# When a gather may start, and whose bytes its rows land in: a hold and a buffer choice in a hybrid encoder block

## The chip, the cores and the metric

One core of one Trainium2 chip runs the whole program. The engines are PE (TensorE: matmuls; its weight loads are listed apart as PEld), DVE (VectorE), ACT (ScalarE), POOL (GpSimd, which also issues the indirect gathers) and SP (SyncE, which issues most other DMAs). Each engine works through its own instructions in a fixed order. The metric is the time of the program on the device, in microseconds; lower is better.

## The reference, cut to what matters

```python
h_res = concat([meta, x])                     # 16 + 1024 tokens of 1024 features
hn = _rmsnorm(h_res, norm_mix)
z = hn @ w_in                                 # all projections
y_m = _mlstm(...)                             # 4 heads of 128, chunk by chunk with a carried state
y_f = _forgetting_attention(...)              # 8 heads of 64
h_res = h_res + concat([y_m, y_f]) @ w_out    # then the 16 meta tokens are dropped
# PEER, for each token, with x = _rmsnorm(h_res, norm_ffn):
#   scores against 2 x 128 keys for each of 8 heads, top 16 of each, top 16 of their pairs
#   -> ids: 8 x 16 = 128 experts of 16384, gate: softmax of their scores
u = u_emb[ids]
act = gelu(einsum('ted,td->te', u, xb))
w = gate * act
out = h_res + einsum('te,ted->td', w, v_emb[ids])
```

Everything is float32.

## The kernel before, in words

The 1024 tokens are cut into four segments of 256 tokens, each of two blocks (A and B) of 128. Each segment passes its projections (`proj`), the mLSTM (`mlstm`), the attention (`fox`), the output projection and the norm (`outp`), and the choice of experts (`topk`: q projection, scores, top 16; eight heads, one after the other, each writing 16 columns of the index tile `idx` and of `gate`). What this text calls the front of a segment is the part up to `outp`. The last instructions of `outp` transpose the normed tokens (`xT`, L858).

The experts are evaluated in two ways. Segments 1 and 2 (512 tokens) are done densely: every expert row is multiplied with every token (`dense_u`, L293, and `dense_v`, L1258), and the gates are scattered into a matrix over all experts (`gates`: 128 groups of four tokens, with one-hot rows A on DVE and ACT, one-hot rows B on POOL and DVE at L1161, their product `gout` on PE at L1163, a copy to `G` on ACT at L1165, and a store `gd`). Segments 0 and 3 gather: for each block, 128 gathers fetch one u row per token each (`gu`, L329: 128 tokens by 1024 floats, 512 KB), DVE (L338) or POOL and ACT (L335, L336) multiply a row with the tokens `xng` and sum it; `weigh` makes the weights with gelu and gate; then 128 gathers, one per token, fetch that token's 128 v rows (`gv`, L365), and `po` (L387) multiplies four of them at a time on PE. Such four gathers are called a four.

`gather_items` gives the order for a gathered segment: all of A's u rows; then in turn a four of A's v rows and four of B's u rows; then B's v rows. `GS0` says which of 16 u rows are multiplied on POOL: rows 2, 5, 8, 11, 14 for block A and none for block B.

A gathered row lands in a buffer of one of two pools. `gp` has 7 and is open from the start. `gpv` has 4; it takes the bytes that the mLSTM's tiles (`vp`, `og`, `mqk`) use, and opens once the mLSTM of the last segment is done. `room0` chooses for segment 0 (L1004): a v row of block A goes to `gpv` from the four with number JV on, one of block B in every second four, all else to `gp`.

The instructions of a program are put in order for each engine by a planner that runs them on a model of the chip ahead of time; among instructions that could go it takes the one that stands first in the program. The gather of segment 0 stands late in the program (`GP0` = 5: after the gates), so its instructions fill what the others leave. In the kernel before, `gather` adds a dependency by hand: the first gather waits for `segs[1].done`, the last transpose of segment 1's `outp`, and all other gathers of the segment are put behind the first.

The program runs in stages. Stage i has the mLSTM of segment i, then, merged, its attention and output projection, the projections of segment i + 1, in stage 1 the top-k of segment 0, and in stage 3 that of segments 1 and 2. After stage 3 come, merged, the top-k of segment 3, part of the dense u products (`spill`) and the gates. The dense phase follows, with the gather of segment 3 paced beside it.

Of the kernel before, what the change touches and what calls it, by code (L numbers as in the profile page):

```python
# [19 lines left out]
P = 128  # L20
# [60 lines left out]
GATH = 7  # L81
GATHV = 4

JV = 4

RATE = 1.08
LAG = 5
# [6 lines left out]
def _block_kernel(ctx, tc, nc, I, out, dbg):  # L94
# [30 lines left out]
    def bank(name):  # L125
        turn_b[0] += 1
        if extra is not None and turn_b[0] % XB == 0:
            return extra[:, turn_b[0] // XB % 2, :]
        return ps.tile([P, 512], F32, tag="bank", name=name, bufs=2)
# [9 lines left out]
    dve, act, pe, pool_e, sync = nc.vector, nc.scalar, nc.tensor, nc.gpsimd, nc.sync  # L139
# [6 lines left out]
    ident = identr.bitcast(F32)  # L146
# [67 lines left out]
    def rsqrt(o, x, scale, t):  # L214

        act.activation(o, x, AF.Ln, bias=epsc[0:x.shape[0]], scale=scale)
        act.activation(o, o, AF.Exp, scale=-0.5)
        act.activation(t, o, AF.Square)
        dve.scalar_tensor_tensor(t, x, EPS / scale, t, op0=OP.add, op1=OP.mult)
        dve.tensor_scalar(t, t, -0.5 * scale, 1.5, op0=OP.mult, op1=OP.add)  # L220
        dve.tensor_mul(o, o, t)
# [32 lines left out]
    def rawt(name):  # L254
        return wp.tile([P, L], F32, tag="raw", name=name, bufs=RAW)
# [8 lines left out]
    for i in range(3):  # L264
        c = slice(i * 512, min(L, i * 512 + 512))
        for e, t in enumerate((oz, zo)):
            t = t[0:NH_F, 0:c.stop - c.start]
# [130 lines left out]
    def gather_items(S, share, room):  # L398

        A, B = (gather_rows(S, lb, share[lb], room) for lb in range(NB))  # L400
        yield from A.u
        for i in range(0, P, 4):
            yield from A.v[i:i + 4]
            yield from B.u[i:i + 4]
        yield from B.v


    def segment(sg):
        S = SimpleNamespace()
        S.sg = sg  # L410
        S.idT = None
        S.nb = nb = SEGS[sg]
        S.xb0 = xb0 = sum(SEGS[:sg])
        S.off = off = NMETA if sg == 0 else 0
        S.nx = nb * P
        S.n = S.nx + off
        S.c0 = 0 if sg == 0 else NMETA + xb0 * P
        S.chunks = ([(0, NMETA)] if sg == 0 else []) + [(off + i * P, P) for i in range(nb)]
        S.hx = len(S.chunks) - nb
        S.xs = slice(xb0 * P, xb0 * P + S.nx)  # L420
        S.T1 = S.c0 + S.n
        return S

    def tok_proj(wsrc, xh, xl, tbs, consume):

        bks = [acc_bank("tk") for _ in tbs]
        for kp in range(4):
            if xl is None:
                raw = rawt("raw")[:, 0:1024]
                sync.dma_start(raw, wsrc[kp])  # L430
                for k in (2 * kp, 2 * kp + 1):
                    for b, (ti, (s0, w)) in zip(bks, tbs):
                        pe.matmul(b[0:w, :], xh[:, k, s0:s0 + w], raw[:, k % 2 * 512:(k % 2 + 1) * 512],  # L433
                                  start=(k == 0), stop=(k == KT - 1))
                continue
            for kk, (h, l) in enumerate(halves(wsrc[kp], SHARE)):
                k = 2 * kp + kk
                for b, (ti, (s0, w)) in zip(bks, tbs):
                    a, c = xh[:, k, s0:s0 + w], xl[:, k, s0:s0 + w]
                    for i, (x, wx) in enumerate(((a, h), (a, l), (c, h))):  # L440
                        pe.matmul(b[0:w, :], x, wx, start=(k == 0 and i == 0), stop=(k == KT - 1 and i == 2))
        for b, (ti, (s0, w)) in zip(bks, tbs):
            consume(ti, w, b)
# [376 lines left out]
    def outp(S):  # L820

        nb, xb0, yh, yl = S.nb, S.xb0, S.yh, S.yl
        if dbg: dbg("yh", S.sg, yh); dbg("yl", S.sg, yl)
        h2p = sp.tile([P, NB, D], F32, tag="u0", name="h2b")
        h2s = [h2p[:, b, :] for b in range(nb)]
        for b in range(nb):
            sync.dma_start(h2s[b], I["x"][(xb0 + b) * P:(xb0 + b + 1) * P, :])
        for nq in range(2):
            def take_w(ti, w, b):
                o = h2s[ti][:, nq * 512:(nq + 1) * 512]  # L830
                dve.tensor_add(o, o, b)
            tok_proj(I["wo"][nq], yh, yl, [(b, (b * P, P)) for b in range(nb)], take_w)
            yield
        gffn = rawt("gffn")[:, 0:D]
        sync.dma_start(gffn, I["g_ffn"].partition_broadcast(P))
        if S.sg <= DENSE[1]:
            half_ = slice((S.sg - DENSE[0]) % 2 * NX, ((S.sg - DENSE[0]) % 2 + 1) * NX)
            xh, xl = Xh[:, :, half_], Xl[:, :, half_]
        else:
            xh = hp.tile([P, KT, NTOK], F32R, tag="hh", name="xh3")[:, :, 0:nb * P]  # L840
            xl = None
        if S.sg in Q32:
            xh, xl = xh.bitcast(F32), None
        S.xh, S.xl = xh, xl
        for b in range(nb):
            gb_ = xb0 + b
            sync.dma_start(h2d[gb_ * P:(gb_ + 1) * P, :], h2s[b])
            xn = rawt("xn")[:, 0:D]
            ssq = sp.tile([P, 3], F32, tag="ssq", name="ssq")
            act.activation(xn, h2s[b], AF.Square, accum_out=ssq[:, 0:1])  # L850
            rsqrt(ssq[:, 1:2], ssq[:, 0:1], 1.0 / D, ssq[:, 2:3])
            dve.scalar_tensor_tensor(xn, h2s[b], ssq[:, 1:2], gffn, op0=OP.mult, op1=OP.mult)
            if S.sg not in DENSE:
                sync.dma_start(xnd[gb_ * P:(gb_ + 1) * P, :], xn)
            for half in range(2):
                tb = bank("xT")
                for i in range(4):
                    S.done = pe.transpose(tb[:, i * P:(i + 1) * P], xn[:, (4 * half + i) * P:(4 * half + i + 1) * P], ident)  # L858
                dsth = xh[:, 4 * half:4 * half + 4, b * P:(b + 1) * P]
                if xl is not None:  # L860
                    dstl = xl[:, 4 * half:4 * half + 4, b * P:(b + 1) * P]
                tbv = tb.rearrange("p (k t) -> p k t", k=4)
                act.copy(dsth, tbv)
                if xl is not None:
                    dve.tensor_sub(dstl, tbv, dsth.bitcast(F32))
        yield
# [111 lines left out]
    segs = [segment(i) for i in range(len(SEGS))]  # L978
    NPROJ, NTOP = 2 + 1 + 8 + 2 + 8, NH_P

    def main(S):
        yield from fox(S)
        yield from outp(S)
# [21 lines left out]
    def room0(kind, lb, i):  # L1005

        if kind == "v":
            return gpv if (i >= JV if lb == 0 else i % 2) else gp
        return gp

    def gather(S, share):
        first = None
        for ask, use in gather_items(S, share, room0):
            with tc.issue_after(first.ins) if first else nullcontext():
                t, d = ask()
            if first is None:
                first = d

                tc.add_manual_dep(d.ins, segs[1].done.ins.name, mybir.DependencyInfo(
                    mybir.DependencyClass.Sync, mybir.DependencyReason.DATA), reason="hold")  # L1020
            more = use(t)
            if more:
                more()

    class Paced:
# [22 lines left out]
        def use(self):  # L1048
            _, f, t = self.open.pop(0)
            with ExitStack() as es:  # L1050
                for k in ("pe", "dve"):
                    if k in seen:
                        es.enter_context(tc.issue_after(seen[k].ins))
                more = f(t)
            if more:
                self.later.append((self.at, more))
# [11 lines left out]
    def gather_first(at):  # L1068
        if GP0 == at:
            gather(segs[0], GS0)  # L1070

    for i in range(-1, len(SEGS)):
# [9 lines left out]
        if i >= 0:  # L1082
            S = segs[i]
# [239 lines left out]
```

## Time and profile before

| what | value |
|---|---|
| median of 3 runs | 3425.85 us (3422.84 to 3432.39) |
| the profiled execution | 3424.24 us, span 3422.4 us |
| mean granted clock of TensorE | 0.926 |
| PE, DVE, ACT, POOL busy | 3040.1, 2294.6, 1066.8, 1523.4 us |
| HBM read, written | 860.91 MB, 67.47 MB |

A line of the page or of an answer of the trace has the line of the kernel, the engine, the operation, the tiles (out<-in) and a count; `[... <-X]` or `<-X` names what ended the idle time before an instruction. In tables by stretch the first figures are the start, end and length of a stretch in microseconds from the start of the span; then each engine's busy microseconds, with the number of its records in brackets; then the granted clock of TensorE as a share of full speed, the mean busy share of the 16 DMA engines and the GB/s they moved. An answer for one tile counts all instructions that write or read it: for `gu` on DVE two records for each row (product and its sum), on POOL the gathers and POOL's own products.

### The profile page before, as it was taken

The numbers are of one execution on the slowest core, as the hardware profiler recorded it, in microseconds if no ns is written. First come the engines' busy times: TensorE is split into PE (matmuls) and PEld (weight loads), VectorE is DVE, ScalarE is ACT, GpSimd is POOL, SyncE is SP. The second block draws the span as 40 slices with busy tenths as digits, with TensorE's granted clock in tenths as the row PEclk, the third lists the DMA queues.
The fourth block names the chain that finished last, engine by engine and source line by source line (L and its number), as shares of the span: only waits on it lengthen the run. The fifth ranks groups of instructions, "written<-read, shape, count | busy, mean of one in ns | idle before, by whom it ended". The sixth has DMA issues, their size and how long they took to land. (4 is left out here: it accounts for less than half of the span.)

```text
span 3422.4 us, 42278 instructions
## 1 busy us (share of the span) xinstructions
PE 3040.1 (89%) x14225; PEld 2220.2 (65%) x14225; DVE 2294.6 (67%) x5970; ACT 1066.8 (31%) x2007; POOL 1523.4 (45%) x1321
## 2 busy tenths in 40 slices
PE   8899899878768868999998775999999999999999
PEld 4566677545535646676766553777777777777666
DVE  3242678577667999776788546788767677775443
ACT  1323424233333212222444553222322232322221
POOL 1000011177875777433565675454444545444442
PEclk9998899879679888999998886999999999999999
DMA  4444445579989999866787887888889999998995
GB/s 135 131 126 137 144 145 149 167 240 315 250 299 331 328 334 346 252 242 234 283 325 280 316 302 284 287 311 314 307 310 344 345 348 343 353 342 308 339 333 205
DMA packets 373821, 931.23 MB, mean 272 GB/s; under 512 B 57268, under 2 KB 143508, under 8 KB 371556
## 3 DMA queue, kind: packets, MB, share of 16 engines
q0 software_dynamic: 161216, 552.56, 45.9%
q1 hardware_dynamic: 212388, 375.96, 32.7%
q8 instruction: 113, 1.85, 0.2%
q14 instruction: 104, 0.85, 0.1%
HBM read 860.91 MB, written 67.47 MB: 271 GB/s over the span
## 5 line engine op out<-in xcount | busy, mean ns | idle before, releaser
L329 POOL DMA_INDIRECT gu<-in_peer_u,idx x512 | 626.3, 1223 | 521.1 <-PE vo L1258 110.0
L365 POOL DMA_INDIRECT gv<-in_peer_v,idT x512 | 546.0, 1066 | 593.1 <-PE po L387 314.3
L338 DVE SCALAR_TENSOR_TENSOR gu<-gu,xng 128x1024 f32<-128x1024 f32 x472 | 592.5, 1274 | 62.5 <-DMA gu<-in_peer_u,idx 60.6
L282 ACT CAST wh<-raw 128x1024 fp32r<-128x1024 f32 x288 | 302.1, 1049 | 884.2 <-PE vo L1258 270.9
L287 DVE TENSOR_TENSOR wl<-raw,wh 128x1024 fp32r<-128x1024 f32 x262 | 320.5, 1223 | 283.0 <-ACT wh L282 250.5
L1258 PE MATMUL vo<-wh,Wh 128*128 128x512 f32 x1024 | 376.7, 396 | 34.9 <-ACT Wh L1239 18.1
L1258 PE MATMUL vo<-wl,Wh 128*128 128x512 f32 x1024 | 402.6, 393 | 0.0
L1258 PE MATMUL vo<-wh,Wl 128*128 128x512 f32 x1024 | 400.3, 392 | 0.0
L387 PE MATMUL po<-gv,Z 128*32 128x512 f32 x2048 | 262.7, 606 | 19.1 <-DMA gv<-in_peer_v,idT 18.9
L306 PE MATMUL fp<-hnh,raw 128*128 128x256 f32 (+1 forms) x1024 | 251.4, 404 | 22.3 <-DVE frs L633 11.3
L1258 PEld LDWEIGHTS vo<-wh,Wh 128*128 128x128 f32 x1024 | 194.1, 190 | 98.3 <-issue 23.3
L293 PE MATMUL du<-xl,wh 128*128 128x512 f32 x640 | 250.3, 391 | 0.0
L293 PE MATMUL du<-xh,wl 128*128 128x512 f32 x640 | 250.2, 391 | 0.0
L293 PE MATMUL du<-xh,wh 128*128 128x512 f32 x640 | 249.8, 390 | 0.0
L306 PEld LDWEIGHTS fp<-hnh,raw 128*128 128x128 f32 x1024 | 203.8, 203 | 60.5 <-DVE frs L633 12.7
L1258 PEld LDWEIGHTS vo<-wl,Wh 128*128 128x128 f32 x1024 | 193.8, 189 | 48.6 <-issue 8.4
L1258 PEld LDWEIGHTS vo<-wh,Wl 128*128 128x128 f32 x1024 | 193.2, 189 | 48.1 <-issue 7.5
L1163 PE MATMUL gout<-A,B 128*128 128x128 f32 x1024 | 164.0, 319 | 67.6 <-POOL B L1161 62.9
L1163 PEld LDWEIGHTS gout<-A,B 128*128 128x128 f32 x1024 | 150.9, 226 | 103.6 <-POOL B L1161 76.6
L1165 ACT COPY G<-gout 128x512 f32<-128x512 f32 x128 | 136.4, 1066 | 202.0 <-PE gout L1163 195.4
L433 PE MATMUL tk<-raw,hnh 128*128 128x512 f32 (+1 forms) x416 | 197.4, 623 | 2.0 <-ACT vp L576 1.8
L1263 DVE TENSOR_TENSOR acc<-acc,vo 128x512 f32<-128x512 f32 x256 | 167.0, 683 | 32.8 <-PE vo L1258 29.1
(409 smaller groups left out, 5397.5 us busy)
## 6 DMA issues: line engine op xcount, KB each, us to landing
raw<-in_ut SPq DMA_DIRECT2D x128, 512.0 KB
raw<-in_peer_v SPq DMA_DIRECT2D x128, 512.0 KB
raw<-in_wf SPq DMA_DIRECT2D x64, 512.0 KB
gd<-G SPq DMA_DIRECT2D x16, 2048.0 KB
Gt<-gd SPq DMA_DIRECT2D x32, 1024.0 KB
raw<-in_wt SPq DMA_DIRECT2D x48, 512.0 KB
raw<-in_wq SPq DMA_DIRECT2D x48, 512.0 KB
raw<-in_wo SPq DMA_DIRECT2D x32, 512.0 KB
```

The costliest lines, as they stand in the source:

```text
L282: seen["act"] = act.copy(h, raw)
L287: seen["dve"] = dve.tensor_sub(l, raw, h.bitcast(F32))
L293: seen["pe"] = pe.matmul(o, w, x[:, c], start=(first and i == 0), stop=(last and i == 2))
L306: pe.matmul(o, raw[:, k * P:(k + 1) * P], xh[:, k, c], start=(k == 0), stop=(k == KT - 1))
L329: d = pool_e.indirect_dma_start(out=t, out_offset=None, in_=I["peer_u"], in_offset=bass.IndirectOffsetOnAxis(ap=S.idx[:, lb, r:r + 1], axi ...
L338: dve.scalar_tensor_tensor(t, t, 1.0, xn[0], op0=OP.mult, op1=OP.mult, accum_out=G.actv[:, r:r + 1])
L365: d = pool_e.indirect_dma_start(out=t, out_offset=None, in_=I["peer_v"], in_offset=bass.IndirectOffsetOnAxis(ap=S.idT[lb][:, tok:tok + 1], ...
L387: last = pe.matmul(G.po[32 * q_:32 * q_ + 32, n, :], z[:, q_, 31 - j:63 - j], rows[q_][:, n * 512:(n + 1) * 512], start=(j == 0), stop=(j ...
L433: pe.matmul(b[0:w, :], xh[:, k, s0:s0 + w], raw[:, k % 2 * 512:(k % 2 + 1) * 512], start=(k == 0), stop=(k == KT - 1))
L1163: pe.matmul(bk[:, u * P:(u + 1) * P], B[:, u, :], A[:, u, :], start=True, stop=True)
L1258: seen["pe"] = pe.matmul(bks[b], w[:, cw], v, start=(ii == 0 and i == 0), stop=(ii == GRP - 1 and i == 2))
L1263: dve.tensor_add(o, o, bks[b])
```

## The change

The manual dependency and the chaining of the gathers behind the first one go, with the attribute `done` that they used. `JV` is 14 in place of 4: block A's values use `gp` for their first 14 fours and `gpv` from the 15th on. The change also has the words that the second block's rows are on VectorE alone; the list for the second block is empty in the kernel before as well, and the diff does not touch it.

```diff
-JV = 4
+JV = 14
...
             for half in range(2):
                 tb = bank("xT")
                 for i in range(4):
-                    S.done = pe.transpose(tb[:, i * P:(i + 1) * P], xn[:, (4 * half + i) * P:(4 * half + i + 1) * P], ident)
+                    pe.transpose(tb[:, i * P:(i + 1) * P], xn[:, (4 * half + i) * P:(4 * half + i + 1) * P], ident)
...
     def gather(S, share):
-        first = None
         for ask, use in gather_items(S, share, room0):
-            with tc.issue_after(first.ins) if first else nullcontext():
-                t, d = ask()
-            if first is None:
-                first = d
-
-                tc.add_manual_dep(d.ins, segs[1].done.ins.name, mybir.DependencyInfo(
-                    mybir.DependencyClass.Sync, mybir.DependencyReason.DATA), reason="hold")
-            more = use(t)
+            more = use(ask()[0])
             if more:
                 more()
```

`room0`, unchanged, reads the constant:

```python
        if kind == "v":
            return gpv if (i >= JV if lb == 0 else i % 2) else gp
        return gp
```

## The prediction

> **What bounds the kernel now.** I read four views: busy time of each engine by stretch, cut at the events of the code; the same stretches for the gathered rows alone (u rows into `gu`, v rows into `gv`); the groups of the stretch where PE idles most; and single instructions in order of time. First, where the gathers start and how far behind their inputs.
>
> ```profile
> 670.89 1.06 POOL L329 DMA_INDIRECT gu<-in_peer_u,idx  x1 [2.61 <-PE xT L858]
> ...
> L951 DVE CAST idx<-idfh x64: 98/174/2720, 410.8 to 1903.9; 128x16 int32<-128x16 f32 x64
> ...
> 649.85 0.17 DVE L951 CAST idx<-idfh 128x16 int32<-128x16 f32 x1
> ...
> 1207.51 0.34 DVE L707 SCALAR_TENSOR_TENSOR Cst<-Cst,dec,mst 128x129 f32<-128x129 f32 x1
> ...
> 1726.77 1.21 DVE L392 TENSOR_TENSOR h2o<-h2o,po 128x1024 f32<-128x1024 f32 x1
> ```
>
> The first gather waits for the transposes L858 of the second front and goes at 670.9 us. Head 0's indices are there at 410.8, head 7's at 649.9. The last state update of the mLSTM is at 1207.5; its bytes become the four `gpv` buffers then. Block A's values end at 1726.8.
>
> All engines, by stretch (busy us, count; then granted clock, DMA share, GB/s):
>
> ```profile
> core 0: us, PE busy (x) PEld busy (x) DVE busy (x) ACT busy (x) POOL busy (x), PEclk, DMA share, GB/s
> 411.00:668.00 257.00, 234.53 (x1157) 179.85 (x1157) 189.63 (x770) 79.96 (x189) 20.05 (x20) 0.93 0.47 137
> 670.00:997.00 327.00, 233.12 (x855) 160.98 (x853) 227.83 (x407) 108.48 (x258) 252.96 (x177) 0.79 0.88 278
> 997.00:1207.00 210.00, 164.85 (x706) 120.33 (x706) 167.22 (x473) 58.14 (x124) 138.84 (x102) 0.88 0.91 323
> 1207.00:1364.00 157.00, 124.97 (x595) 94.01 (x596) 155.63 (x532) 33.10 (x60) 117.15 (x94) 0.84 1.02 339
> 1364.00:1640.00 276.00, 260.64 (x1275) 182.95 (x1274) 192.23 (x763) 69.73 (x118) 99.20 (x87) 0.96 0.74 250
> 1731.00:1904.00 173.00, 159.35 (x931) 116.42 (x930) 150.96 (x624) 74.23 (x147) 106.45 (x103) 0.94 0.83 311
> 1904.00:2110.00 206.00, 137.95 (x829) 98.24 (x828) 113.68 (x318) 107.89 (x219) 151.94 (x143) 0.80 0.80 299
> ```
>
> PE is the bound before the gathers (91% in 411-668), again in 1364-1640 (94%) and 1731-1904 (92%). It idles 94 us of 327 while u rows run, 32 us in 1207-1364, where DVE is full (155.6 of 157), and 68 us in 1904-2110. The same stretches for the u rows:
>
> ```profile
> core 0: us, DVE busy (x) ACT busy (x) POOL busy (x), PEclk, DMA share, GB/s
> 670.00:997.00 327.00, 120.69 (x170) 42.46 (x74) 242.80 (x163) 0.79 0.88 278
> 997.00:1207.00 210.00, 90.73 (x142) 3.45 (x6) 103.70 (x78) 0.88 0.91 323
> 1207.00:1364.00 157.00, 69.05 (x110) 0.00 (x0) 68.61 (x55) 0.84 1.02 339
> ```
>
> On POOL the first count is 123 gathers and 40 products, the others gathers alone; so 123, 78 and 55 u rows. One row costs DVE 69.05/55 = 1.26 us. And for the v rows (POOL's count is rows):
>
> ```profile
> core 0: us, PE busy (x) PEld busy (x) POOL busy (x), PEclk, DMA share, GB/s
> 997.00:1207.00 210.00, 7.70 (x64) 1.67 (x64) 17.90 (x16) 0.88 0.91 323
> 1207.00:1364.00 157.00, 11.54 (x96) 2.50 (x96) 34.58 (x28) 0.84 1.02 339
> 1364.00:1640.00 276.00, 32.70 (x272) 7.09 (x272) 74.67 (x74) 0.96 0.74 250
> 1640.00:1731.00 91.00, 13.19 (x80) 2.49 (x80) 21.16 (x20) 0.98 0.74 269
> 1731.00:1904.00 173.00, 35.02 (x240) 7.72 (x240) 61.36 (x61) 0.94 0.83 311
> 1904.00:2110.00 206.00, 38.39 (x272) 7.87 (x272) 57.44 (x57) 0.80 0.80 299
> ```
>
> Sixteen v rows (the four fours of JV = 4) pass before 1207, the other 240 after it, and 57 only after 1904, when the projections and top-k of the last segment are done and just the gates remain. The groups of that tail (busy us, mean ns; idle before, who ended it):
>
> ```profile
> line engine op names shapes xcount | busy us, mean ns | idle before us <-releasers
> L1163 PE MATMUL gout<-A,B 128*128 128x128 f32 x537 | 98.0, 348 | 62.2 <-POOL B L1161 57.6 <-issue 4.0 <-ACT A L1157 0.6
> ...
> L1161 POOL TENSOR_SCALAR B<-iota,jT,gT 128x128 f32<-128x128 f32 x67 | 71.9, 1076 | 22.4 <-PE gout L1163 20.6 <-DMA gv<-in_peer_v,idT 0.5 <-POOL B L1161 0.2
> L1165 ACT COPY G<-gout 128x512 f32<-128x512 f32 x68 | 71.8, 1055 | 95.2 <-PE gout L1163 93.8 <-issue 0.5
> L1161 DVE TENSOR_SCALAR B<-iota,jT,gT 128x128 f32<-128x128 f32 x201 | 62.8, 373 | 0.2 <-issue 0.2
> L365 POOL DMA_INDIRECT gv<-in_peer_v,idT x57 | 57.4, 1008 | 26.5 <-PE po L387 14.2 <-issue 9.7 <-PE gout L1163 2.3
> ...
> L1153 DVE TENSOR_TENSOR A<-iota,iT 128x384 f32<-128x384 f32 x67 | 37.6, 561 | 76.5 <-PE gout L1163 75.4 <-issue 0.7
> L1156 ACT ACTIVATE A<-iota,niT 128x128 f32<-128x128 f32 x67 | 26.4, 394 | 0.0
> L329 POOL DMA_INDIRECT gu<-in_peer_u,idx x19 | 23.0, 1213 | 4.7 <-issue 3.4 <-DVE B L1161 0.5 <-DVE A L1153 0.5
> L1157 ACT ACTIVATE A<-A 128x128 f32<-128x128 f32 x67 | 19.6, 310 | 1.4
> ```
>
> POOL's busy and idle times there add to the whole tail: 71.9 + 22.4 + 57.4 + 26.5 + 23.0 + 4.7 = 205.9 of 206 us. PE's longest wait is for POOL's B (57.6 us), and B stands in POOL's queue behind v gathers, some of which wait for a buffer that `po` on PE frees (14.2 us). POOL's queue sets the tail.
>
> **The change, part by part.** The sum is made against the profiled execution, 3424.2 us (span 3422.4); the median of the three runs is 1.6 us above.
>
> *1. The hold goes.* No instruction goes with it; A's u gathers are no longer chained one behind the other either, and their next input is the index column. Does a gather wait for its head or for all eight? The program tracks parts of a tile: the gate matmuls start on the first of eight `hnh` slices while later ones are still to be written:
>
> ```profile
> 392.47 1.05 PE L483 MATMUL gb<-hnh,wgr 128*72 128x256 f32 x4 [2.74 <-issue]
> ...
> 394.34 1.67 DVE L470 SCALAR_TENSOR_TENSOR hnh<-hraw,gmix,rstd 128x256 f32<-128x256 f32 x4
> ```
>
> So gathers start near 411, not 671. DVE has 257 - 190 = 67 us idle in 411-668. A's rows take DVE 11/16 of the time and POOL 5/16, so a full DVE would take 67/1.26/(11/16) = 77 rows; none would be the other end. I take 55, since the indices come a head at a time.
>
> What 55 rows cost there: with 123 rows PE idled 94 of 327 us; at the 9% of 411-668 it would have idled 29; 65/123 = 0.53 us a row, hence 55 x 0.53 = **+29 us** (ends: 0, if they fit into DVE's idle time, and +130, worked out with the first rival). What they give back later: A's other 73 rows at the rate of 670-997 (123 in 327 us) end near 864; then fours of A's values and of B's u rows alternate, 184 rows until B's u rows are through, at the rate of 997-1207 (94 in 210 us): to 1275 in place of 1364. So 670-1207 has 30 u rows fewer, 30 x 0.53 = 16 us, and 1207-1364 has 25 of its 55 fewer. DVE fills that stretch; without any u row PE would bound it, 125 us at 94% being 132 of 157, so 25/55 of 25 are 11 us. Together **-27 us** (ends: 0, and -61, if PE lost all its 45 idle us of 997-1207 and 16 more).
>
> *2. JV from 4 to 14.* Forty more rows of A's values use `gp`, which is open from the start, in place of `gpv`. No instruction is added; ten fours of `po`, 32.70/(272/16) = 1.92 us each, move ahead of 1207, into PE's idle time. If that cover were gone they would cost 19 us. They take buffers from B's u rows, which is counted in the 184 rows above; all 56 are through by 864 + 112/0.448 = 1114, before `gpv` opens.
>
> After 1207, 200 v rows are left in place of 240. A's last 72, on `gpv` alone, at the rate of 1364-1640 (74 rows in 276 us): 269 us, to 1476. B's 128 at the rate of 1731-1904 (61 in 173): 363 us, to **1839** in place of the tail. The PE-bound time 1207-1904 gets 200 in place of 183 rows, 17 x 1.92/4 = **+8 us**.
>
> *3. The tail without v rows.* POOL loses 57.4 + 26.5 = 84 us: 122 remain. ACT needs 1.055 + 0.394 + 0.310 = 1.76 us for each of 67 groups: 118. DVE needs 0.561 + 3 x 0.373 = 1.68 a group, PE 98 in all. So the tail is 118 to 126 us in place of 206; I take 126, **-80 us**. Its next limit is ACT with POOL, no longer the gathers. The ends are -88 and 0 (the v rows still there). The 19 early u gathers of the last segment may go sooner; they are in POOL's 122.
>
> *4. The second block on VectorE alone.* Its list of POOL shares is empty in both kernels: no change.
>
> *Queues passed.* POOL's gathers now stand before the `kqa` loads and the `wl` products of 411-668 (20 us of POOL work), in order; a gather whose index is late holds these up, and so the attention. SP's load of `xng` for block B moves with the end of A's rows; its wait stands before weight loads.
>
> Sum: +29 - 27 + 8 - 80 = -70, so 3424.2 - 70 = 3354, and on the median's level **3356 us** (-2.0%).
>
> A row on which I could have decided otherwise, min/median/max of one row's product on each engine:
>
> ```profile
> L338 DVE SCALAR_TENSOR_TENSOR gu<-gu,xng x472: 1190/1217/3821, 677.3 to 3086.9; 128x1024 f32<-128x1024 f32 x158
> ...
> L335 POOL TENSOR_TENSOR gu<-gu,xng x40: 2343/2358/2775, 682.0 to 1012.7; 128x1024 f32<-128x1024 f32 x40
> ```
>
> By these medians 55 rows bring DVE 38 x 1.26 = 48 us, 238 of 257: no stretch of the stage by DVE alone. The longest DVE product is 2.6 us over the median, about one POOL product. [...]
>
> **The rivals.** *Slower: the second front pays more than the tail gives.* Place: 411-668, where PE was at 91% undisturbed; mechanism: gathers wait for indices in POOL's order, DVE fills, PE's gaps lower the granted clock. If it ran like 670-997, which did 233 x 0.79/327 = 0.56 us of full-clock PE work per us, its 234.5 x 0.93 = 218 us would take 387, +130. With -27, +8 and -80: 3455 us. It decides from +99 on. For it: 0.93 against 0.79 of clock with and without u rows. Against: 670-997 holds twice the rows and a serial mLSTM too. [...]
>
> *No change.* The written order leaves the v rows among the gates (they come last in the program in both kernels), or the front's price takes up the tail's gain. Time 3424, within 10. For it: v rows have 65 us to spare at 1904, from rates alone. Against: 40 rows fewer wait for 1207.
>
> *Faster still.* The rows fit into DVE's idle time, so +29 is 0, and a quarter of PE's 45 idle us in 997-1207 goes too: 3315 us.
>
> **How the numbers follow.** Forecast 0.55 (own range 3330 to 3400), faster still 0.14, no change 0.12, slower 0.19. Faster by over 0.3% (10 us, about what a measurement of this kernel tells from nothing) is 0.55 + 0.14 = 0.69. The range 3295 to 3440 reaches past the fast case and most of the way to the slow one.
>
> **What would show it.** The first gather near 411 in front of L858; about 55 u rows by 668 (by its end); PE's share there in the eighties; 72 v rows left on `gpv`; h2o of block A near 1450 and of B before the top-k ends; in the tail no L365 on POOL, PE's wait for B under 20 us, about 1.9 us a group. It is wrong if v gathers still stand between the B's, or if the second front grows by about 100 us. A short front with a full tail would mean that the order, not the buffers, places the values.

## The result, and the profile after

The changed kernel takes 3370.95 us (median of 4 runs, 3361.7 to 3375.85) against 3428.85 us before (4 runs too, among them the three that gave 3425.85): a ratio of 0.983, 95% interval 0.9802 to 0.9857. The forecast was 3356. The stages below are read from one profiled execution of each kernel; the spans of these, 3422.4 and 3374.1 us, are 48 us apart, the medians 58.

Both kernels by stage: to the last transpose of the second front, of the third, of the fourth, to the last product of the gates, and to the end. First before, then after:

```profile
core 0: us, PE busy (x) PEld busy (x) DVE busy (x) ACT busy (x) POOL busy (x), PEclk, DMA share, GB/s
371.00:671.00 300.00, 270.73 (x1324) 207.82 (x1323) 221.36 (x899) 103.94 (x251) 23.04 (x22) 0.91 0.46 135
671.00:1054.00 383.00, 270.42 (x987) 181.73 (x985) 254.81 (x459) 125.23 (x294) 285.01 (x203) 0.79 0.88 283
1054.00:1636.00 582.00, 508.71 (x2425) 373.11 (x2425) 488.09 (x1710) 142.59 (x263) 322.11 (x258) 0.91 0.87 293
1636.00:2110.00 474.00, 384.20 (x2264) 281.92 (x2262) 339.41 (x1241) 224.22 (x451) 304.25 (x289) 0.89 0.80 299
2110.00:3422.30 1312.30, 1270.97 (x5996) 958.20 (x5994) 861.66 (x1273) 360.42 (x462) 562.65 (x493) 0.99 0.89 319
```

```profile
378.00:784.00 406.00, 294.06 (x1319) 222.52 (x1318) 375.23 (x1047) 137.84 (x310) 235.93 (x166) 0.83 0.74 244
784.00:1135.00 351.00, 283.63 (x1185) 178.29 (x1184) 201.03 (x455) 92.37 (x232) 194.33 (x176) 0.84 0.95 316
1135.00:1683.00 548.00, 509.89 (x2622) 365.42 (x2621) 412.87 (x1594) 144.32 (x266) 271.47 (x237) 0.95 0.87 292
1683.00:2055.00 372.00, 312.10 (x1876) 250.30 (x1875) 328.94 (x1222) 218.36 (x450) 229.19 (x193) 0.93 0.65 247
2055.00:3374.00 1319.00, 1276.09 (x5999) 961.72 (x5997) 858.83 (x1265) 360.99 (x463) 566.19 (x493) 0.98 0.89 317
```

The second front grew by 106 us, the next two shrank by 32 and 34, the stage of the gates by 102. (The first stage and the last, which the change does not touch, are 7 us longer each; between the profiles of this study the first varies from 370 to 379.) Where the gathers went, after: the first one, and POOL's work in the second front:

```profile
419.06 2.90 POOL L329 DMA_INDIRECT gu<-in_peer_u,idx  x1 [3.75 <-DVE idx L951]
```

```profile
L329 POOL DMA_INDIRECT gu<-in_peer_u,idx x113 | 132.4, 1172 | 110.2 <-DVE gu L338 30.9 <-issue 15.2 <-DVE Zm L755 14.8
L335 POOL TENSOR_TENSOR gu<-gu,xng 128x1024 f32<-128x1024 f32 x34 | 81.9, 2408 | 2.0 <-DMA gu<-in_peer_u,idx 1.4
```

The first gather waits for its head's indices, as forecast, and 113 u rows pass in the front, not 55. The v rows (busy time of PE, PEld and POOL; POOL's count is rows):

```profile
1135.00:1683.00 548.00, 69.52 (x592) 16.27 (x592) 158.07 (x159) 0.95 0.87 292
1683.00:1920.00 237.00, 33.35 (x208) 6.77 (x208) 43.40 (x42) 0.98 0.72 268
1920.00:2055.00 135.00, 0.00 (x0) 0.00 (x0) 0.00 (x0) 0.85 0.53 209
```

The last is issued at 1819 us in place of 2063, so none is left among the last gates. The groups of the stretch from 1917 on (lines 8 lower than before):

```profile
L1155 PE MATMUL gout<-A,B 128*128 128x128 f32 x510 | 81.9, 311 | 51.2 <-POOL B L1153 45.6 <-DVE A L1145 3.4 <-issue 0.7
L1153 POOL TENSOR_SCALAR B<-iota,jT,gT 128x128 f32<-128x128 f32 x62 | 80.6, 1304 | 27.4 <-PE gout L1155 23.7 <-ACT gT L1128 2.6 <-PE idt L360 0.5
```

These are 64 groups in 138 us. But the last top-k ends at 1989 here (1904 before), so the stretch also holds the end of that top-k and, on POOL, 19 u gathers of the last segment. Behind 1989 stand 40 groups, in 66 us, with neither:

```profile
L1153 POOL TENSOR_SCALAR B<-iota,jT,gT 128x128 f32<-128x128 f32 x40 | 46.7, 1173 | 19.3 <-PE gout L1155 16.1 <-ACT gT L1128 2.6 <-PE idt L360 0.5
L1155 PE MATMUL gout<-A,B 128*128 128x128 f32 x323 | 46.7, 287 | 19.5 <-POOL B L1153 17.7 <-issue 0.7 <-ACT G L1157 0.6
```

### The profile page after: what moved, and what is told of

Same layout as the page of the kernel before. It is cut to its first block, busy times and chain, and to the rows that moved or that the text cites. A ratio compares the mean times of both kernels' runs of the same rounds, so it can differ in the third digit from the quotient of the medians.

```text
span 3374.1 us, 42267 instructions
## 1 busy us (share of the span) xinstructions
PE 3018.2 (89%) x14225; PEld 2199.6 (65%) x14225; DVE 2306.3 (68%) x5970; ACT 1063.9 (32%) x2007; POOL 1523.5 (45%) x1321
## 4 chain that ended last, share of the span: by engine, by line
PE 61%; DVE 18%; DMA 7%; issue 7%; POOL 4%; ACT 2%; SPq 0%; POOLq 0%; ACTq 0%; DVEq 0%
PE vo L1250 18%; PE du L293 10%; PE po L387 7%; PE fp L293 6%; DVE gu L338 5%; PE tk L433 5%; PE fp L306 4%; DMA gu<-in_peer_u,idx 2%; PE q L293 2%; DMA gv<-in_peer_v,idT 2%; POOL gu L329 2%; PE pv L787 2%; PE gout L1155 2%; PE fs L774 1%; POOL B L1153 1%
## 5 line engine op out<-in xcount | busy, mean ns | idle before, releaser
L329 POOL DMA_INDIRECT gu<-in_peer_u,idx x512 | 605.2, 1182 | 640.2 <-DVE gu L338 168.2
L338 DVE SCALAR_TENSOR_TENSOR gu<-gu,xng 128x1024 f32<-128x1024 f32 x472 | 593.8, 1274 | 111.0 <-DMA gu<-in_peer_u,idx 109.6
L306 PE MATMUL fp<-hnh,raw 128*128 128x256 f32 (+1 forms) x1024 | 258.4, 411 | 38.1 <-DVE frs L633 20.4
L1153 POOL TENSOR_SCALAR B<-iota,jT,gT 128x128 f32<-128x128 f32 x128 | 151.7, 1189 | 114.1 <-PE gout L1155 93.6
L1155 PE MATMUL gout<-A,B 128*128 128x128 f32 x1024 | 148.6, 294 | 53.0 <-POOL B L1153 45.6
L1155 PEld LDWEIGHTS gout<-A,B 128*128 128x128 f32 x1024 | 134.4, 202 | 75.4 <-POOL B L1153 57.1
```

Of the source, the lines that this page charges most:

```text
L306: pe.matmul(o, raw[:, k * P:(k + 1) * P], xh[:, k, c], start=(k == 0), stop=(k == KT - 1))
L329: d = pool_e.indirect_dma_start(out=t, out_offset=None, in_=I["peer_u"], in_offset=bass.IndirectOffsetOnAxis(ap=S.idx[:, lb, r:r + 1], axi ...
L338: dve.scalar_tensor_tensor(t, t, 1.0, xn[0], op0=OP.mult, op1=OP.mult, accum_out=G.actv[:, r:r + 1])
L1153: e.tensor_scalar(B[:, u, :], iota, jT[:, t1], gT[:, t1], op0=OP.is_equal, op1=OP.mult)
L1155: pe.matmul(bk[:, u * P:(u + 1) * P], B[:, u, :], A[:, u, :], start=True, stop=True)
```

## The experiments

All runs in one table: medians, ratio to the kernel before on the same chip with its interval, and from each trace the length of the four middle stages and the issue of the last v row of segment 0 (us). e3, e5 and e8 leave out part of the result, to price what they leave out; the others compute all of it.

| run | us | ratio | front 2 | front 3 | front 4 | gates | last v |
|---|---|---|---|---|---|---|---|
| before | 3429 | 1 | 300 | 383 | 583 | 474 | 2063 |
| changed | 3371 | 0.983 (0.980-0.986) | 406 | 351 | 548 | 372 | 1819 |
| e1_jv_only | 3427 | 1.000 (0.998-1.001) | 300 | 384 | 594 | 448 | 2016 |
| e2_no_hold_only | 3390 | 0.989 (0.987-0.991) | 406 | 351 | 500 | 446 | 2003 |
| e4_48_free | 3380 | 0.986 (0.985-0.988) | 341 | 363 | 585 | 401 | 1917 |
| e3_short_products | 3342 | 0.976 (0.975-0.978) | 359 | 334 | 580 | 373 | 1793 |
| e5_all_short | 3269 | 0.954 (0.951-0.956) | 308 | 325 | 552 | 392 | 1749 |
| e6_more_pool | 3414 | 0.997 (0.995-0.999) | 413 | 369 | 552 | 381 | 1852 |
| e7_no_pool | 3348 | 0.978 (0.975-0.981) | 363 | 365 | 520 | 402 | 1823 |
| e8_fewer_values | 3364 | 0.981 (0.978-0.984) | 300 | 384 | 589 | 402 | 1916 (of 200) |
| f1_before_no_pool | 3336 | 0.972 (0.969-0.975) | 300 | 317 | 581 | 436 | 1992 |
| f2_hold_no_pool_jv14 | 3353 | 0.977 (0.975-0.980) | 297 | 313 | 617 | 436 | 1953 |
| f3_no_pool_no_share | 3314 | 0.967 (0.964-0.969) | 377 | 346 | 522 | 373 | 1760 |
| f4_no_pool_at_all | 3308 | 0.964 (0.961-0.968) | 377 | 348 | 526 | 363 | 1766 |

**Each part alone.** First theory: the buffers (JV) make the tail's gain, the free start makes the front's cost. e1 edits the kernel before, e2 the changed kernel:

```diff
 # e1: hold kept          # e2: hold gone
-JV = 4                   -JV = 14
+JV = 14                  +JV = 4
```

> The hold as before, JV 14. Theory (the buffers of A's values make the tail's gain, the free start makes the front's cost): second front 300 us as before, 383 and about 582 us for the two stages after it, tail 370 in place of 474: 3320 to 3335 us, faster than both kernels. Rival (the early start makes the tail's gain): tail 450 to 474, 3400 to 3425 us.

> No hold, JV 4. Theory: front 406, then 351 and 548 as in the changed kernel, but 112 of A's v rows still wait for the mLSTM's bytes and the tail stays over 430: 3425 to 3465 us, not faster than before. Rival (early start makes the tail's gain): tail 370, 3360 to 3375 us.

The theory fell, twice. JV alone does nothing: 40 of A's v rows in `gp` take the places of B's u rows, whose last gather slips from 1363 to 1509 us, so that the last v row comes only 47 us earlier, and 25 v rows still go after the last top-k (second row; the first is the stage of the gates):

```profile
1651.00:2098.00 447.00, 76.61 (x496) 15.73 (x496) 119.34 (x118) 0.92 0.78 290
1931.00:2098.00 167.00, 21.04 (x144) 4.21 (x144) 25.11 (x25) 0.84 0.70 264
```

The free start alone does about two thirds of the gain: its front is the dear one of 406 us, but the third front falls by 32 us, the fourth by 83, as B's u rows end at 1131, and the gates by 28. JV 14 on top of it lengthens that front again (500 to 548) and shortens the gates more (446 to 372). The rival was half right: the start earns, but most of it in the fronts, not in the tail.

**What the front pays for.** The rows were dosed, in the kernel before with JV 14:

```diff
-JV = 4
+JV = 14
+
+FREE = 48
...
-            if first is None:
+            if n == FREE:   # the 49th gather waits for the second front
```

> JV 14; the first 48 u rows go freely, the 49th waits for the second front. If a row costs the front the same 0.94 us wherever (106/113), the front is 345 us and some 28 us come back after it: 15 to 20 us slower than JV alone. If the first rows fit into VectorE's idle 67 us, the front is under 320 and the total at or below that of JV alone.

48 rows cost 41 us, 113 rows 106: 0.85 and 0.94 us a row, from the first row on. That the first rows fit into VectorE's idle time is refuted; for the front the linear case is borne out. For the total it is not: at 3380 us e4 is 47 below JV alone (e1), not 15 to 20 above it, because the third front, the fourth and the gates give back 21, 9 and 47 us against e1, far more than the 28 expected. Then the products of the changed kernel were cut, VectorE's first, POOL's and ACT's with them next:

```diff
-                dve.scalar_tensor_tensor(t, t, 1.0, xn[0], ...)
+                c = slice(0, 32 if S.sg == 0 and lb == 0 else D)
+                dve.scalar_tensor_tensor(t[:, c], t[:, c], 1.0, xn[0][:, c], ...)
...                                              # e5 also:
-                pool_e.tensor_tensor(t, t, xn[0], op=OP.mult)
+                pool_e.tensor_tensor(t[:, c], t[:, c], xn[0][:, c], op=OP.mult)
-                return lambda: act.activation(t, t, AF.Copy, ...)
+                return lambda: act.activation(t[:, c], t[:, c], AF.Copy, ...)
```

> The changed kernel with VectorE's products of block A of segment 0 over 32 of 1024 columns (part of the u sums is left out); gathers and POOL's products stay. Theory (VectorE's time makes the front's cost): some 78 products of 1.24 us go from the front, which falls from 406 to 300-320 us; total 3270 to 3300 us. Rival (POOL's order and the DMA make it): front stays over 375, total 3340 to 3370 us.

> As the run with short VectorE products, and POOL's products and ACT's sums of block A over 32 columns too (their sums are partly left out); the gathers stay. Theory (a POOL product holds VectorE's instructions: L947 went from 570 to 843 ns in the front): the front falls from 359 to 305-325 us and L947 to about 600 ns. Rival (the gathers themselves, by issue order and DMA): the front stays over 345 us and L947 over 680 ns.

Short VectorE products gave 359 us, between the theories: 47 of the 106 us (the total, 3342, lies in the rival's range). With POOL's products and ACT's sums short too, the front is back at 308 (e5):

```profile
373.00:681.00 308.00, 268.03 (x1319) 204.36 (x1318) 226.72 (x1045) 108.45 (x309) 144.90 (x164) 0.92 0.91 312
```

112 gathers pass in that stretch, the DMA share is 0.91 in place of 0.46, and PE keeps its clock (0.92; 0.91 before). So the DMA traffic and POOL's order of gathers cost 8 us, short products included. The full products cost the rest: 47 us went with VectorE's and 51 with those on POOL, an engine that the front hardly used before (23 us), and the sums on ACT that follow them. How they cost, the same instructions of VectorE in the second front show: first in the kernel before, then in the changed one, then in e7, which has no products on POOL:

```profile
L947 DVE TENSOR_TENSOR oh<-iota,posf 128x400 f32<-128x400 f32 x32 | 18.2, 570 | 0.5
L950 DVE TENSOR_REDUCE idfh<-oh 128x8 f32<-128x400 f32 x32 | 18.0, 563 | 0.5
L594 DVE SCALAR_TENSOR_TENSOR mqk<-rawc,taps,mqk 128x256 f32<-128x256 f32 x24 | 11.3, 475 | 0.1
L220 DVE TENSOR_SCALAR fsq<-fsq 128x256 f32<-128x256 f32 x9 | 2.6, 288 | 0.1
```

```profile
L338 DVE SCALAR_TENSOR_TENSOR gu<-gu,xng 128x1024 f32<-128x1024 f32 x75 | 111.0, 1482 | 10.6 <-DMA gu<-in_peer_u,idx 10.6
L947 DVE TENSOR_TENSOR oh<-iota,posf 128x400 f32<-128x400 f32 x32 | 27.0, 843 | 0.2
L950 DVE TENSOR_REDUCE idfh<-oh 128x8 f32<-128x400 f32 x32 | 17.9, 559 | 0.3
L594 DVE SCALAR_TENSOR_TENSOR mqk<-rawc,taps,mqk 128x256 f32<-128x256 f32 x24 | 16.3, 687 | 0.1
L220 DVE TENSOR_SCALAR fsq<-fsq 128x256 f32<-128x256 f32 x9 | 10.0, 1107 | 0.1
```

```profile
L338 DVE SCALAR_TENSOR_TENSOR gu<-gu,xng 128x1024 f32<-128x1024 f32 x114 | 143.8, 1265 | 12.0 <-DMA gu<-in_peer_u,idx 11.8
L947 DVE TENSOR_TENSOR oh<-iota,posf 128x400 f32<-128x400 f32 x32 | 18.1, 567 | 0.1
L594 DVE SCALAR_TENSOR_TENSOR mqk<-rawc,taps,mqk 128x256 f32<-128x256 f32 x24 | 11.1, 468 | 0.0
L220 DVE TENSOR_SCALAR fsq<-fsq 128x256 f32<-128x256 f32 x9 | 2.5, 283 | 0.0
```

Three instructions of unchanged shape go from 570 to 843, from 475 to 687 and from 288 to 1107 ns beside POOL's products, the reduction (563, 559) does not grow, and without POOL's products the three are back (567, 468 and 283 ns) while as many gathers run. Single records of the changed front show it too: one L594, 474 ns at the median, takes 3.11 us from 503.36, across a product of POOL of 2.37 us from 503.81; one L220, 282 ns at the median, takes 5.36 us from 657.97, across a `wl` product and a row's product that follow each other on POOL from 658.48 to 663.16. The longest of the 32 reductions takes 571 ns. What decides which instructions grow, no run shows.

The front feels it through PE's waits for VectorE. The longest two, before and after:

```profile
PE fp L306 <- DVE frs L633: 8.2, 2, 5.8
PE xT L858 <- DVE xn L852: 4.8, 1, 4.8
```

```profile
PE xT L858 <- DVE xn L852: 21.9, 1, 21.9
PE fp L306 <- DVE frs L633: 17.1, 3, 10.5
```

PE idled 29 us of the front before and 112 after, 83 of the 106 us; the other 23 are busy time at a granted clock of 0.83 in place of 0.91. All waits of PE for VectorE add up to 22 us before and 95 after. A rival is ACT, whose sums wait for POOL's products in order (85 us of idle time in this front) and may hold up its other work: PE's waits for ACT add up to 4 us before and 15 after, so it is a small part at most; no run varies the sums alone.

**Who multiplies.** In the changed kernel (e6, e7), and in the one before (f1, f2):

```diff
-GS0 = ((2, 5, 8, 11, 14), ())
+GS0 = ((1, 3, 5, 7, 9, 11, 13, 15), ())   # e6
+GS0 = ((), ())                            # e7, f1, f2 (f2 also JV = 14)
```

> The changed kernel with 8 of 16 of block A's products on POOL in place of 5. If only VectorE's own product time counts, 113 x 3/16 x 1.26 = 27 us leave VectorE and the front is 380 us, the total near 3350. If POOL's products hold VectorE, nothing is won: front 400 to 420 us, total 3370 to 3390.

> The changed kernel with all of block A's products on VectorE. If only VectorE's own product time counts, 34 products x 1.26 = 43 us come to a full VectorE: front 430 to 450 us, total 3390 or more. If POOL's products hold VectorE, some 60 us of stretch go: front 385 to 405 us, total 3350 to 3375, L947 back near 600 ns.

More products on POOL made every stage from the second front to the gates slower (front 413), and the total, 3414, more than the 3370 to 3390 expected. None on POOL made it faster (3348; the intervals of this ratio and of the change's overlap by 0.001) though VectorE, busy 375 of 406 us already, took 39 more: front 363, of 119 rows, 0.53 us a row, less than the holding theory had expected (385 to 405). VectorE was busy 375 us with 75 products in the changed kernel and is 338 us with 114 here:

```profile
373.00:736.00 363.00, 283.44 (x1329) 216.87 (x1328) 337.87 (x1124) 102.56 (x246) 169.12 (x138) 0.86 0.82 278
```

So the changed front has 37 us more of busy VectorE and 39 products fewer, 48 us at the median of 1.22 us each: by an estimate from these, its VectorE lost 85 us against e7. POOL's 34 products there took 81.9 us.

> The kernel before (hold, JV 4) with all of block A's products on VectorE. If POOL's products held VectorE in the stage after the second front too, where 40 of them ran, that stage falls from 383 to 345-360 us and the total to 3385-3405. If the free start was needed for that (only the front was short of VectorE), no change: 3415 to 3435 us.

> The same with JV 14. If the free start earns by itself, this is slower than the free start without POOL's products (3348) by 20 us or more, 3370 to 3400 us, with v rows still in the tail. If POOL's products were all that mattered, 3340 to 3360 us.

f1 beats the change (3336 against 3371) with one line and the hold in place, and the expected 3385 to 3405 too. Most of its gain is in the third front, where the 40 products ran: 383 to 317 us, more than expected (345-360). The gates fall by 38 us as well (474 to 436), and the dense stage is 18 longer.

```profile
674.00:991.00 317.00, 248.20 (x988) 170.96 (x987) 242.80 (x541) 85.86 (x215) 192.23 (x166) 0.86 1.02 343
```

The groups of that front, before and in f1:

```profile
L338 DVE SCALAR_TENSOR_TENSOR gu<-gu,xng 128x1024 f32<-128x1024 f32 x95 | 134.2, 1431 | 40.4 <-DMA gu<-in_peer_u,idx 39.4 <-ACT rawc L589 0.9
L594 DVE SCALAR_TENSOR_TENSOR mqk<-rawc,taps,mqk 128x256 f32<-128x256 f32 x24 | 19.7, 821 | 0.5
```

```profile
L338 DVE SCALAR_TENSOR_TENSOR gu<-gu,xng 128x1024 f32<-128x1024 f32 x136 | 163.9, 1219 | 21.0 <-DMA gu<-in_peer_u,idx 20.5
L594 DVE SCALAR_TENSOR_TENSOR mqk<-rawc,taps,mqk 128x256 f32<-128x256 f32 x24 | 11.5, 482 | 0.4
```

As many rows are multiplied (95 on VectorE and 40 on POOL before, 136 on VectorE in f1), and VectorE is busy 243 us in place of 255. f2 (3353) stands with e7 (3348), not 20 us above it: with JV 14 and the products off POOL, the free start earns nothing that these runs show (with JV 4 it was not run so), and JV 14 costs 16 us against f1 in the same set of runs (front 4 is 617 in place of 581).

**The tail's price by itself.** The kernel before without 56 of block B's v rows:

```diff
-        yield from B.v
+        yield from (B.v if S.sg else B.v[:56] + B.v[112:])
```

> The kernel before without 56 of block B's 128 v gathers of segment 0 and their po matmuls (that part of the output is left out), so that hardly any v row is left after the last top-k. Theory (v rows in POOL's queue set the tail): the tail 474 falls to 385-400 us, the last part of it to about 1.7 us a group of gates, total 3335 to 3350. Rival (the tail is the gates' own, by ACT and PE): under 30 us gained.

The stage of the gates falls by 72 us; the second and third fronts are as they were, the fourth is 6 us longer, and the total, 3364, is 14 above the range expected. The 72 us are the price of all that these rows bring, their `po` on PE and their traffic too, since e8 does not move them but leaves them out. In 1906-2048, after the last top-k, four v rows are left, and its 67 groups take 142 us, 2.1 a group, not 1.7:

```profile
1906.00:2048.00 142.00, 5.77 (x48) 1.25 (x48) 4.77 (x4) 0.90 0.59 228
```

```profile
L1163 PE MATMUL gout<-A,B 128*128 128x128 f32 x536 | 84.2, 308 | 47.8 <-POOL B L1161 42.7 <-issue 2.6 <-ACT G L1165 1.1
L1161 POOL TENSOR_SCALAR B<-iota,jT,gT 128x128 f32<-128x128 f32 x65 | 79.0, 1219 | 26.1 <-PE gout L1163 22.5 <-ACT gT L1136 2.6 <-issue 0.3
```

PE still waits 43 us for POOL's B. In POOL's queue 19 u gathers of the last segment (24.5 us) still stand there; where none stands, after 1989 in the changed kernel, the 40 groups take 1.65 us each and PE's wait is 17.7 us.

**Further off POOL**, on top of e7:

```diff
-SHARE = 3      # every third wl on POOL
+SHARE = 0      # f3, f4
-GPOOL = 1      # one B in four on POOL
+GPOOL = 0      # f4
```

> Free start, JV 14, no POOL products, and the low halves of the weights (wl, every third on POOL) all on VectorE. If every POOL instruction with two operands holds VectorE as the row products did, VectorE gains more than the 26 x 1.2 us it takes on: 3325 to 3342 us. If it is their own time that counts, 3350 to 3370 us.

> The same with the gates' B on VectorE alone too (one in four was on POOL, one SBUF operand beside per-partition scalars). If POOL held VectorE there as well, 5 to 20 us faster than without it. If not, VectorE gets 128 x 0.37 = 47 us more of its own, and the stage of the gates grows: 10 to 40 us slower.

f3 is at 3314, under the forecast of the holding theory. In its fourth front, where e7 still has 17 of the `wl` products on POOL, the mean of L947 is 566 ns and 681 in e7; but that stage is as long (522 and 520), and the gain on e7 stands in the third front (365 to 346) and the gates (402 to 373), while the second front, with all 128 rows, grew (363 to 377). How much of it is holding is not shown. f4, 3308, is the fastest run that computes the whole result (0.964 of before); its 6 us on f3 lie within the intervals, so whether B on POOL held VectorE stays open. These two with the hold and JV 4, as f1 suggests, were not run.

## Why the prediction was right or wrong

The time was right, 15 us off, but by luck: its terms were not right, and they made up for each other. The forecast had +29, -27, +8 and -80 us; the profiles have +106 in the second front, -66 in the third and fourth, -102 in the gates and +14 in the first and last stage.

- **The first gather** (part 1): right, at 419, by head.
- **The front, +29**: wrong, +106, and by the forecast's own sign (a second front that grows by about 100 us) its account was wrong there. PE was busy 72% of it, not in the eighties. Two sizes failed. 113 rows went there, not 55: the step that capped them by VectorE's idle time failed, for the order let them in and the front grew. And a row cost 0.94 us, not 0.53. The step behind this is the reading of L338's row: I worked with the median of the kernel before, though the longest product was 2.6 us above it, and left what POOL's products cost VectorE inside a price measured elsewhere. That median (1217 ns) counts 472 products, of which only 95 ran in the third front, where POOL multiplied; their mean was 1431 ns. In the changed front the median does not move either (1214 ns, minimum, median and maximum below), while the mean of the same products is 1482:

```profile
L338 DVE SCALAR_TENSOR_TENSOR gu<-gu,xng x75: 1198/1214/4205, 426.3 to 783.4; 128x1024 f32<-128x1024 f32 x75
```

In this front POOL's products with their sums were half the cost (51 us went with them, 47 with VectorE's products). Without them the row costs 0.53 us (e7), but the forecast's 0.53 came from a stretch with 40 of them in it, so that these agree is chance.

- **What comes back, -27, with the +8 for v rows moved there**: -66 us. Twice the rows left the later stages, but so did 34 of POOL's 40 products, and f1 shows that taking all 40 out of the third front gives 66 us there; which of the two did it here is not shown.
- **JV 14** (part 2): its own dates held in the changed kernel (56 v rows by 1078, forecast 1114; B's u rows to 1249, forecast 1275; last v 1819, forecast 1839). That the 40 rows take buffers from B's u rows stood there, and that it decides without the free start did not: e1.
- **The tail, -80**: 72 us where the rows are left out (e8), 102 for the stage of the gates in the changed kernel. The forecast's 126 us for 67 groups after the last top-k was 142 in e8, with POOL's B at 1219 ns in place of 1076. In the changed kernel that top-k ends 85 us later and only 40 groups stand behind it; there both signs came true, 1.65 us a group (1.9 said) and 17.7 us of PE's wait for B (under 20 said). Over its last 64 groups, with the u gathers of the last segment among them, it is 2.2 us a group and 46 us.
- **The slower rival** was nearer on the front (+130) than the forecast: the measured +106 passed the +99 from which it was to decide. It did not, because 47 us more came back in the next two fronts than the -27 and +8 had, and 22 more in the gates. The clock fell as it said, 0.91 to 0.83, with PE idle 112 of 406 us in place of 29 of 300; that the gaps lower it was an estimate from such stretches, and no run varies the gaps alone. The faster rival fell with e4.

## What to carry to other kernels

Compare the mean of one unchanged instruction between stages: where it grows beside another engine's work (here 288 to 1107 ns), that work is not free, however idle its engine looks (POOL, busy 45% of the span), and taking it back can pay even on a full engine (e7: 0.978 of the kernel before in place of the change's 0.983, with VectorE busy 375 of 406 us in the changed front). Run each part of a change alone before a gain is put down to one of them; here the part that seemed to earn earned nothing alone. A median hides what befalls fewer than half of the instructions (1214 ns here, the mean 1482): take the mean, over the stretch in question. A price for each row, taken from one stage, holds in another only if the neighbours are alike.

## What the runs showed of the hardware that was not expected

Beside 34 products of two operands on POOL (2.4 us each) a VectorE `tensor_scalar` took nearly four times as long in the changed front (288 to 1107 ns on average over nine; 283 without these products, e7). Moving 40 such products (94 us of an engine busy 45% of the span), with their sums on ACT, to one busy 67% made the kernel 2.8% faster (f1; interval of the ratio 0.969 to 0.975). 112 indirect gathers of 512 KB beside a front in which PE is busy 268 of 308 us, without full products, cost it 8 us (e5).
